# A hybrid encoder layer: the second sequence is scaled on ScalarE and transposed by channel tile, key rows are rotated after the fetch, weight splits are joined, and the output's products stand in another order

## The chip, the cores and the metric

The kernel runs on one core of a Trainium2 chip. The metric is the device time of one execution, in microseconds (us). TensorE is called PE, VectorE DVE, ScalarE ACT, GpSimd POOL and SyncE SP; SP issues nearly all DMAs, in order.

## The reference: what is computed

One encoder layer, for two independent sequences (a prompt and a sample) of 512 tokens and 1024 channels, all in float32.

```python
h = rms_norm(x, pre_g)
z = h @ w_in                                   # 6,560 columns, split into the parts below
(u_pool, c_q, kv_a, u_conv, u_four, g_pool, g_attn, g_conv, g_four, z_merge) = split(z)
y_pool = pool_mixer(u_pool, pool_w, pool_scale) * silu(g_pool)
y_attn = mla(c_q, kv_a, q_norm_g, w_uq, kv_norm_g, w_ukv) * silu(g_attn)   # 8 heads, rope on 32 key channels
y_conv = conv_module(u_conv, ...) * silu(g_conv)                          # 31 taps, layer norm, product
y_four = fourier_mixer(u_four, fourier_w) * silu(g_four)
gates = sigmoid((z_merge + gate_b).reshape(B, S, 4, D))
m = sum(gates[:, :, i] * (y_i @ w_up_i) for the four branches)
return x + rms_norm(m @ w_out, post_g)
```

## The kernel before

**Products.** Every product is made in three passes over numbers split in a high and a low half (`split`: ACT writes the high half, rounded to fp32r, then DVE or POOL subtracts it from the source and writes the low one); `mm3` issues the three passes, so that 8 channel tiles are 24 matmul instructions. Matmuls are up to 512 columns wide.

**Two sequences in one product.** Sequence 0 (F in the code) and sequence 1 (G) are taken together: the input projection has 50 channel tiles of 128, taken as 25 `PAIRS`, and each pair makes its 2 x 2 blocks (two channel tiles, two sequences) with seven products instead of eight. `group_units` names them `m1` to `m7`. Their right factors are the halves (channels 0 to 511, and 512 to 1023) of the hidden rows, transposed: B11 and B21 of sequence 0, B12 and B22 of sequence 1, and the sums T1 = B12 - B11, T2 = B22 - T1, T3 = B22 - B12, T4 = B21 - T2. `m1` and `m2` need sequence 0 alone, `m6` needs T2, and `m5`, `m7`, `m4`, `m3` need T1, T3, T4 and B22. Each left factor is a weight tile or a sum of weight tiles, split in the same way (`into`). The output product with `w_out` has seven products as well (`out_product(1)` to `(7)`, with left factors by `LEFT`, and `out_sums` for the sums of the merged rows).

**The front.** For each token tile of 128, `a_units` loads the rows, squares them (`stat`), scales them by the norm and the gain (`norm`), and transposes eight channel tiles on PE (`turn`). `b_units` is the projection on the query and key latents (416 columns wide, four tiles for each sequence); its evacuation norms them, rotates the 32 key channels (rope), and spills 480 columns to DRAM (`st`). The group stream follows, and beside it run the taps of the convolution: 120 DVE instructions on PSUM. Then come the attention, whose rows are fetched from DRAM by `c_units`, the merges (`merges(n)` for four branches), and the output, ended for each token tile by `half_out`, `residual` and `final`.

**The order.** A recorder keeps every instruction with what it reads and writes. `schedule` lists the bulk of PE's work in program order and gives the rest ("sides") start and end times from the table `PLAN`, relative to marks in the bulk. A planner then orders all instructions of each engine by these due times, an estimate of their durations, and the buffers that are free. `either` leaves it to the planner whether DVE or POOL takes an operation, `copied` whether ACT or DVE does. All DMAs stand in SP's order. Because the recorder issues every instruction at one place, all have line L182 in the profile, and groups are told apart by their tiles (`b` and `g` are SBUF buffers, `ps` PSUM, `s` small columns, `st` spilled rows, `in_wt` the projection's weights, `in_wv` the value weights).

The bulk around the output before the change:

```python
bulk.extend(out_product(1) + [out_gains()] + out_product(2))
merges(3, 1)
bulk.extend(out_sums(k) for k in range(4))
for n in (6, 7, 5):
    bulk.extend(out_product(n))
```

## Time and profile before

| what | value |
| --- | --- |
| median of 3 runs | 953.57 us |
| all runs | 953.54, 953.57, 1499.98 us |
| the profiled execution | 957.25 us |
| its span | 955.4 us |
| PE busy | 905.9 us (95%), 4,128 instructions |
| DVE, ACT, POOL busy | 724.1, 484.3 and 363.3 us |
| DMA | 130.90 MB in 55,842 packets |
| PE idle | 49.5 us |

The profile covers one execution; its span is from the first instruction to the last, and the execution's own time has 1.85 us around it. Times in rows are microseconds from the span's start. A row of the timeline has the start, the length, the engine, the line, the operation, the tiles written and read, and the number of instructions that were taken together; in brackets, how long the engine had been idle and what ended that.

### The profile page before, as it was taken

What the parts mean: (1) busy time and instruction counts of PE and PEld (TensorE: products, weight loads), DVE (VectorE), ACT (ScalarE), POOL (GpSimd) and SP (SyncE); (2) the same over time, 40 slices, a digit from 0 to 9 for tenths busy, and PEclk for the clock granted to TensorE, in tenths of its full rate; (3) what the DMA queues carried; (4) which work ended last, traced back from release to release, by engine and by line L of the source; (5) the groups of instructions that cost most, each with busy time, mean ns of one, the idle gap of its engine ahead of it and who ended that gap; (6) DMA issues with size and microseconds to landing.
All of it is one profiled execution on the core that took longest, in us unless ns stands there. A gap on an engine that the chain in (4) does not pass through costs nothing. (4 is left out here: it accounts for less than half of the span.)

```text
span 955.4 us, 12309 instructions
## 1 busy us (share of the span) xinstructions
PE 905.9 (95%) x4128; PEld 731.4 (77%) x4128; DVE 724.1 (76%) x1129; ACT 484.3 (51%) x907; POOL 363.3 (38%) x332
## 2 busy tenths in 40 slices
PE   5969999999999999999999998999999899999895
PEld 5967877877788887878888886878778677777684
DVE  5997999989655446477444375688989888888997
ACT  6734333334544544344444364665657787763343
POOL 4998433524212013142011021332533153359974
PEclk9998999999999999999999999899999999999898
DMA  7204024222343226335334234857842762640134
GB/s 276 99 32 153 14 99 142 90 109 99 133 155 121 78 69 212 122 111 187 105 138 137 94 117 118 278 187 244 285 151 67 224 238 80 220 143 22 43 113 176
DMA packets 55842, 130.90 MB, mean 137 GB/s; under 512 B 6882, under 2 KB 10211, under 8 KB 55267
## 3 DMA queue, kind: packets, MB, share of 16 engines
q1 hardware_dynamic: 55778, 130.13, 40.8%
q8 instruction: 32, 0.52, 0.2%
q14 instruction: 32, 0.25, 0.1%
HBM read 89.34 MB, written 37.62 MB: 133 GB/s over the span
## 5 line engine op out<-in xcount | busy, mean ns | idle before, releaser
L182 PE MATMUL ps<-b,b 128*128 128x512 f32 (+4 forms) x3476 | 824.7, 394 | 24.3 <-ACT b L182 10.2
L182 PEld LDWEIGHTS ps<-b,b 128*128 128x128 f32 (+2 forms) x3476 | 641.3, 189 | 175.4 <-ACT b L182 11.1
L182 DVE TENSOR_TENSOR b<-b,b 128x512 fp32r<-128x512 f32 (+4 forms) x187 | 169.0, 921 | 64.2 <-ACT b L182 60.4
L182 ACT ACTIVATE b<-b 128x512 fp32r<-128x512 f32 (+5 forms) x230 | 150.6, 673 | 125.4 <-PE ps L182 84.2
L182 POOL TENSOR_TENSOR b<-b,b 128x512 fp32r<-128x512 f32 (+3 forms) x82 | 123.3, 1515 | 166.0 <-ACT b L182 107.9
L182 ACT ACTIVATE g<-ps 128x512 f32<-128x512 f32 (+5 forms) x116 | 63.4, 549 | 132.8 <-PE ps L182 115.9
L182 DVE TENSOR_TENSOR g<-ps,g 128x512 f32<-128x512 f32 (+3 forms) x101 | 66.2, 658 | 74.8 <-ACT g L182 40.2
L182 DVE TENSOR_TENSOR b<-ps,b 128x512 fp32r<-128x512 f32 (+2 forms) x126 | 83.9, 682 | 9.4 <-ACT b L182 8.0
L182 ACT ACTIVATE b<-g 128x512 fp32r<-128x512 f32 x101 | 62.0, 628 | 49.4 <-DVE g L182 21.6
L182 DVE SCALAR_TENSOR_TENSOR ps<-b,half,ps 128x512 f32<-128x512 f32 x116 | 84.5, 750 | 1.6
L182 ACT ACTIVATE b<-ps 128x512 fp32r<-128x512 f32 (+2 forms) x117 | 67.8, 592 | 18.0 <-PE ps L182 15.9
L182 POOL TENSOR_TENSOR b<-g,b 128x512 fp32r<-128x512 f32 x37 | 52.0, 1411 | 53.2 <-ACT b L182 37.2
L182 POOL TENSOR_TENSOR b<-b,g 128x512 f32<-128x512 f32 x30 | 42.4, 1416 | 61.2 <-DVE g L182 47.4
L182 DVE TENSOR_TENSOR b<-g,b 128x512 fp32r<-128x512 f32 x64 | 51.3, 810 | 16.4 <-ACT b L182 16.0
L182 ACT ACTIVATE g<-g,half 128x512 f32<-128x512 f32 x48 | 34.8, 725 | 42.7 <-DVE g L182 42.6
L182 ACT ACTIVATE g<-ps,s 128x512 f32<-128x512 f32 x64 | 43.8, 685 | 24.7 <-DVE s L182 17.4
L182 POOL TENSOR_TENSOR b<-b 128x512 f32<-128x512 f32 (+2 forms) x25 | 33.0, 1320 | 39.4 <-DVE g L182 16.6
L182 PE MATMUL ps<-ident,g 128*128 128x128 f32 x280 | 43.0, 275 | 3.5 <-DVE b L182 2.2
L182 DVE TENSOR_REDUCE s<-ps 128x1 f32<-128x512 f32 x64 | 43.5, 682 | 2.5 <-PE ps L182 2.2
L182 DVE TENSOR_TENSOR b<-b 128x512 f32<-128x512 f32 (+4 forms) x50 | 38.6, 774 | 7.9 <-DMA b<-st 2.4
L182 PEld LDWEIGHTS ps<-ident,g 128*128 128x128 f32 x280 | 34.2, 141 | 13.6 <-issue 2.7
L182 POOL TENSOR_TENSOR g<-b,b 128x512 f32<-128x512 f32 x16 | 22.9, 1436 | 51.9 <-DMA b<-in_wt 21.3
(72 smaller groups left out, 567.4 us busy)
## 6 DMA issues: line engine op xcount, KB each, us to landing
st<-g SPq DMA_DIRECT2D x104, 256.0 KB, 2.1
b<-in_wt SPq DMA_DIRECT2D x50, 512.0 KB, 4.2
g<-st SPq DMA_DIRECT2D x100, 256.0 KB, 3.6
b<-in_x SPq DMA_DIRECT2D x15, 512.0 KB, 4.3
b<-in_wup SPq DMA_DIRECT2D x14, 512.0 KB, 5.8
b<-st SPq DMA_DIRECT2D x4, 1024.0 KB, 7.2
b<-in_wo SPq DMA_DIRECT2D x8, 512.0 KB, 4.5
out_y<-b SPq DMA_DIRECT2D x16, 256.0 KB, 2.0
```

The source lines that it names most:

```text
L182: getattr(engines[atom.eng], method)(*[real(x) for x in args], **{k: real(x) for k, x in kw.items()})
```

## The change

The change touches several parts, and all numbers of `PLAN` but a few are new.

1. *Sequence 1's rows.* `norm` scales them in place on ACT by the row's factor alone, without the gain. The new `turn1(k)` transposes the four token tiles of one channel tile into one PSUM bank, and its evacuation (`scaled_`, on ACT or DVE) multiplies by that channel's gain, which is a column of the new tile `gains`; T1 and T3 are made from 512 contiguous columns, and `sums(k)` makes T2 and T4 by channel tile too. `gains` is loaded by a DMA with channels on partitions.
2. *Powers.* The add ahead of a power moves from POOL to DVE, and the two powers of a latent tile are joined to one of two columns; the mean's factor goes into the Square's scale.
3. *Key rows* are spilled unrotated, 416 columns wide; `cn()` in `c_units` rotates all four token tiles at once after the fetch.
4. *Weights.* The two tiles of a pair are loaded into one buffer with their halves side by side, and split 1024 columns at a time (`ga`, `gb`, `gc`) and once 512 (`gd`).
5. *Group stream.* The first pair's `m1` and `m2` are put ahead of sequence 1's latent projection explicitly (`gl=1`).
6. *Output.* Product 7 comes first, on `s3`, made by `out_s3` as the last branch is merged; its four steps alternate with the sums; then come 6, which adds to two sums, 5, 4, 3.
7. *The end.* For sequence 0's last two token tiles, one DVE instruction replaces an ACT scale and an addition.

The diff's core:

```diff
+    def scaled_(out, x, c):
+        rec.choice(act=("activation", (out, x, AF.Copy), dict(scale=c)),
+                   dve=("tensor_scalar", (out, x, c, None), dict(op0=ALU.mult)))
...
-    def rsqrt_(out, ss, inv_n, eps):
+    def rsqrt_(out, ss, eps):
         n = ss.shape[-1]
         t = s_(n)
-        pool.tensor_scalar(t, ss, inv_n, eps, op0=ALU.mult, op1=ALU.add)
+        dve.tensor_scalar(t, ss, eps, None, op0=ALU.add)
         pool.tensor_tensor(out, t, mhalf[:, :n], op=ALU.pow)
...
+        def turn1(k):
+            def fn():
+                h, kk = divmod(k, 4)
+                name, sum_ = ("B12", "T1") if h == 0 else ("B22", "T3")
...
+                for tt in range(4):
+                    pe.transpose(pt[:, tt * P:(tt + 1) * P], st["x", tt][:, k * P:(k + 1) * P], ident)
+                scaled_(b, pt, gains[:, k:k + 1])
+                split(*row_of(name, kk), b)
+                if h == 0:
+                    hi, lo = row_of("B11", kk)
+                    either(t, hi.bitcast(F32), lo.bitcast(F32), ALU.add)
+                    either(t, b, t, ALU.subtract)
+                    st["b", kk] = b, t
+                else:
+                    either(t, b, st["b", kk][0], ALU.subtract)
+                    st["b", kk] = b, st["b", kk][1]
+                split(*row_of(sum_, kk), t)
+            return Unit(fn, 0.43)
...
             def norm():
+                if s:
+                    act.activation(st["x", tt], st["x", tt], AF.Copy, scale=st["rs", tt])
+                    return
...
-                dve.tensor_tensor(cn[:, 384:416], p[:, 384:416], kcs[:, tt, 0, :], op=ALU.mult)
...
-                dve.tensor_copy(cn[:, 432:448], cn[:, 384:400])
-            return [part(j) for j in range(4)] + [Unit(lambda: spill((s, "cn", tt), st.pop(("cn", tt))[:, :480]))]
+                copied(cn[:, 384:416], p[:, 384:416])
+                scaled_(cn[:, :256], p[:, :256], rs[:, 0:1])
+                scaled_(cn[:, 256:384], p[:, 256:384], rs[:, 1:2])
+            return [part(j) for j in range(4)] + [Unit(lambda: spill((s, "cn", tt), st.pop(("cn", tt))[:, :416]))]
...
             def cn():
...
+                k, u = t[:, :, 384:416], t[:, :, 448:480]
+                either(u[:, :, :16], t[:, :, 400:416], kcs[:, :, 1, :16], ALU.mult)
+                either(u[:, :, 16:], t[:, :, 384:400], kcs[:, :, 1, 16:], ALU.mult)
+                either(k, k, kcs[:, :, 0, :], ALU.mult)
+                either(k, k, u, ALU.add)
+                copied(t[:, :, 416:432], t[:, :, 400:416])
+                copied(t[:, :, 432:448], t[:, :, 384:400])
...
-        return (prod("ga0", "B11", "x", True, copy("m1")), prod("ga1", "B21", "y", True, total("m1", 0, i)),
-                prod("gb0", "T2", "x", False, copy("u2")), prod("gc0", "T1", "z", True, lambda p: None),
...
+        return (prod("ga", 0, "B11", "x", True, copy("m1")), prod("ga", 512, "B21", "y", True, total("m1", 0, i)),
+                prod("gb", 0, "T2", "x", False, copy("u2")), prod("gb", 512, "T1", "z", True, lambda p: None),
...
-    LEFT = {1: ("m", 0, 0), 2: ("m", 0, 1), 3: ("m", 0, 1), 4: ("m", 1, 1), 5: "s1", 6: ("m", 0, 0), 7: ("m", 1, 0)}
+    LEFT = {1: ("m", 0, 0), 2: ("m", 0, 1), 3: ("m", 0, 1), 4: ("m", 1, 1), 5: "s1", 6: ("m", 0, 0), 7: "s3"}
...
+                R["s1"] = R["m", 1, 0]
             a11, a12, a21, a22 = [R["m", s, i][:, k, :] for s in range(2) for i in range(2)]
-            s1 = R["s1"][:, k, :]
-            either(s1, a21, a22, ALU.add)
-            either(a21, a11, a21, ALU.subtract)
-            either(a11, s1, a11, ALU.subtract)
+            either(a21, a21, a22, ALU.add)
+            either(a11, a21, a11, ALU.subtract)
             either(a12, a12, a11, ALU.subtract)
...
-        elif n == 6:
-            dve.tensor_tensor(U[1][:, tt, :], p, U[1][:, tt, :], op=ALU.add)
...
+        elif n == 6:
+            for u in (U[7], U[1]):
+                dve.tensor_tensor(u[:, tt, :], p, u[:, tt, :], op=ALU.add)
...
         merges(3, 1)
-        bulk.extend(out_sums(k) for k in range(4))
-        for n in (6, 7, 5):
+        for k in range(4):
+            bulk.insert(marks_c[k] + k, out_s3(k))
+        us = out_product(7)
+        for k in range(4):
+            bulk.extend([out_sums(k), us[k]])
+        for n in (6, 5):
             bulk.extend(out_product(n))
...
+        side("tr1", "start", [G["turn1"](k + h) for k in range(4) for h in (0, 4)])
...
+        sync.dma_start(gains, a["pre"].rearrange("(k p) -> p k", p=P))
```

The instruction order of three places, before and after. PE, behind the latent projections of both sequences, with `ps_247_832` the second product of pair 0 (`m2`), and `b_244_820` and `b_249_852` the halves of T2; before:

```order
L182 MATMUL ps_247_832<-b_132_237,b_196_508 128x512
L182 MATMUL ps_247_832<-b_128_229,b_196_508 128x512 x2
L182 MATMUL ps_247_832<-b_132_237,b_196_508 128x512
L182 MATMUL ps_247_832<-b_128_229,b_196_508 128x512
L182 MATMUL ps_233_761<-b_244_820,b_260_897 128x512
L182 MATMUL ps_233_761<-b_249_852,b_260_897 128x512
L182 MATMUL ps_233_761<-b_244_820,b_260_897 128x512 x2
```

After, the last latent projection is `ps_242_772`; what follows are T1's product of pair 0 and the two first products of pair 1, whose left factor is `b_243_779`:

```order
L182 MATMUL ps_242_772<-b_138_265,b_207_565 128x416
L182 MATMUL ps_251_822<-b_211_581,b_185_481 128x512
L182 MATMUL ps_251_822<-b_216_606,b_185_481 128x512
L182 MATMUL ps_251_822<-b_211_581,b_185_481 128x512 x2
L182 MATMUL ps_251_822<-b_216_606,b_185_481 128x512
L182 MATMUL ps_251_822<-b_211_581,b_185_481 128x512 x2
```

Of the products that follow, these are the last rows of pair 1, and then the first of T2's product (`ps_205_556`, with T2 in `b_260_867` and `b_262_874`):

```order
L182 MATMUL ps_263_876<-b_132_238,b_243_779 128x512
L182 MATMUL ps_263_876<-b_128_230,b_243_779 128x512 x2
L182 MATMUL ps_263_876<-b_132_238,b_243_779 128x512
L182 MATMUL ps_263_876<-b_128_230,b_243_779 128x512
L182 MATMUL ps_205_556<-b_260_867,b_185_481 128x512
L182 MATMUL ps_205_556<-b_262_874,b_185_481 128x512
```

Before, T2's product stood right behind these; now 36 instructions stand between.

SP's queue around the value weights `in_wv`; before, where `b_611` and `b_624` are the query rows:

```order
L182 DMA st_176<-g_597_4462 128x512
L182 DMA b_611_4544<-b_608_4516 32x1024 x2
L182 DMA b_611_4544<-b_611_4544 64x1024
L182 DMA st_177<-g_609_4527 128x512
L182 DMA st_178<-g_614_4580 128x512
L182 DMA b_611_4544<-b_608_4516 32x1024 x2
L182 DMA b_624_4628<-b_608_4516 32x1024 x2
L182 DMA b_624_4628<-b_624_4628 64x1024
L182 DMA b_624_4628<-b_608_4516 32x1024 x2
L182 DMA b_642_4700<-in_wv 128x256
L182 DMA b_527_3742<-in_dft 128x516
```

After:

```order
L182 DMA b_671_4326<-in_wh 128x768
L182 DMA g_672_4335<-st_149 128x512
L182 DMA st_175<-g_663_4283 128x512
L182 DMA b_678_4371<-in_wh 128x768
L182 DMA st_176<-g_676_4360 128x512
L182 DMA b_678_4371<-in_wv 128x256
L182 DMA st_177<-g_679_4374 128x512
L182 DMA b_687_4421<-b_682_4388 32x1024 x2
L182 DMA b_687_4421<-b_687_4421 64x1024
L182 DMA st_178<-g_688_4427 128x512
L182 DMA b_687_4421<-b_682_4388 32x1024 x2
```

The value weights stood behind seven copies of query rows (`b<-b`); now they stand ahead of these.

DVE's last rows, for the last token tiles of sequence 0, with `g_1271_7203` and `g_1363_7136` the output's gain; before:

```order
L182 TENSOR_TENSOR b_1331_7434<-b_1331_7434,g_1271_7203 128x512
L182 TENSOR_TENSOR b_1331_7434<-ps_1430_8048,b_1331_7434 128x512
L182 SCALAR_TENSOR_TENSOR b_1331_7434<-b_1331_7434,s_1461_8319,b_1337_7465 128x512
L182 TENSOR_TENSOR b_1391_7697<-b_1391_7697,b_1337_7465 128x512
L182 TENSOR_TENSOR b_1331_7434<-b_1331_7434,g_1271_7203 128x512
L182 SCALAR_TENSOR_TENSOR b_1331_7434<-b_1331_7434,s_1463_8331,b_1296_7291 128x512
L182 TENSOR_TENSOR b_1391_7697<-b_1391_7697,b_1296_7291 128x512
```

After:

```order
L182 TENSOR_SCALAR s_1536_8205<-s_1480_7629 128x1
L182 TENSOR_TENSOR b_1404_7308<-b_1404_7308,g_1363_7136 128x512
L182 TENSOR_TENSOR b_1404_7308<-ps_1506_7912,b_1404_7308 128x512
L182 SCALAR_TENSOR_TENSOR b_1471_7590<-b_1471_7590,s_1537_8209,b_1413_7346 128x512
L182 SCALAR_TENSOR_TENSOR b_1404_7308<-b_1404_7308,s_1537_8209,b_1413_7346 128x512
L182 TENSOR_SCALAR s_1538_8216<-s_1481_7634 128x1
L182 TENSOR_TENSOR b_1404_7308<-b_1404_7308,g_1363_7136 128x512
L182 SCALAR_TENSOR_TENSOR b_1471_7590<-b_1471_7590,s_1539_8220,b_1410_7330 128x512
L182 SCALAR_TENSOR_TENSOR b_1404_7308<-b_1404_7308,s_1539_8220,b_1410_7330 128x512
```

The last tile's addition with the residual (`TENSOR_TENSOR`, the last row before) became a `SCALAR_TENSOR_TENSOR` that scales as well, and the power's add (`TENSOR_SCALAR s`) now stands on DVE.

More of the change, by code (lines that the diff above doesn't have):

```diff
@@ L532, in trunk_kernel @@
     cols, mhalf = cols[:, :107], cols[:, 107:]
-    half = const((P, 107), F32, "half")
+    gains = const((P, KD), F32, "gains")
     kcs = const((P, 4, 2, 32), F32, "kcs")
@@ L547, in trunk_kernel @@
         srcs["q", j] = (a["wq"][j], 832)
-    for i in range(50):
-        srcs["z", i] = (a["wt"][i], 1024)
     for i in range(10):
@@ L640, in fn, with row_of, sums @@
+        def row_of(name, k):
+            return [x[:, k, :] for x in R[name]]
+        def sums(k):
+            def fn():
+                if k == 0:
                     R["T2"], R["T4"] = [[b_([4, S], F32R), b_([4, S], F32R)] for _ in range(2)]
-                (t2, t1), t4 = st["b", tt], whole("B21", tt)
+                (t2, t1), t4 = st["b", k], g_()
+                hi, lo = row_of("B21", k)
+                either(t4, hi.bitcast(F32), lo.bitcast(F32), ALU.add)
                 either(t2, t2, t1, ALU.subtract)
-                split(*part_of("T2", tt), t2)
+                split(*row_of("T2", k), t2)
@@ L673, in fn @@
                 def fn():
-                    name = "B22" if k0 else "B12"
-                    if tt == 0 and s:
-                        R[name], R["T3" if k0 else "T1"] = [[b_([4, S], F32R), b_([4, S], F32R)] for _ in range(2)]
-                        if k0:
-                            st["hh"], st["hl"] = zip(R["B12"], R["B22"])
-                    elif tt == 0 and k0 == 0:
+                    if tt == 0 and k0 == 0:
                         hidden()
@@ L955, in fn @@
                 t = g_() if t is None else t
-                act.activation(t, p, AF.Tanh, scale=0.5, bias=half[:, GB + b * 8 + c:GB + b * 8 + c + 1])
+                act.activation(t, p, AF.Tanh, scale=0.5, bias=cols[:, GB + b * 8 + c:GB + b * 8 + c + 1])
                 spill((s, "g", b, c), t, act)
@@ L986, in fn @@
                     for j in js:
-                        w = half[:, CWT + c * 31 + j:CWT + c * 31 + j + 1]
+                        w = cols[:, CWT + c * 31 + j:CWT + c * 31 + j + 1]
                         if j == 0:
@@ L1039, in fn @@
                     t, y = g_(), g_()
-                    lg, lb = half[:, LG + c:LG + c + 1], half[:, LB + c:LB + c + 1]
+                    lg, lb = cols[:, LG + c:LG + c + 1], cols[:, LB + c:LB + c + 1]
                     act.activation(t, pt, AF.Tanh, scale=lg, bias=lb)
@@ L1258, in fn @@
                 v, w = st["half", 1 - q, tt], st["half", q, tt]
-                act.activation(v, v, AF.Copy, scale=r)
-                either(v, v, st["xr", tt][1 - q], ALU.add)
+                if s == 0 and tt > 1:
+                    dve.scalar_tensor_tensor(v, v, r, st["xr", tt][1 - q], op0=ALU.mult, op1=ALU.add)
+                else:
+                    act.activation(v, v, AF.Copy, scale=r)
+                    either(v, v, st["xr", tt][1 - q], ALU.add)
                 dve.scalar_tensor_tensor(w, w, r, st["xr", tt][q], op0=ALU.mult, op1=ALU.add)
@@ L1368, in whole, with prod @@
             evac(0, i2)(p)
-        def prod(key, r, bank, first, then):
+        def prod(key, o, r, bank, first, then):
             def part(j):
@@ L1519, in side @@
             sides.append((marks[mark] + t, marks[mark] + t + n, us))
-        def direct(s, n):
-            for i in PAIRS[n]:
-                bulk.extend(Fs[s]["z"](i, Fs[s]["tile"](i)))
         def merges(n, *ss):
@@ L1542, in schedule @@
         at("groups")
-        ln = [f["ln"]() for f in Fs]
-        late = [u for n in range(nd, len(PAIRS)) for i in PAIRS[n] for u in Fs[1]["z"](i, Fs[1]["tile"](i))]
-        bulk.extend(group_stream(range(nd), lambda n: [u for i in range(2) if n == q["pw%d" % i] for u in ln[i][1]], late))
+        bulk.extend(rest)
         at("tail")
@@ L1560, in schedule @@
         side("a1", "start", stagger(au1))
-        side("sums", "start", [G["sums"](tt) for tt in range(4)])
+        side("tr1", "start", [G["turn1"](k + h) for k in range(4) for h in (0, 4)])
+        side("sums", "start", [G["sums"](k) for k in range(4)])
         for s, F in enumerate(Fs):
@@ L1599, in const_unit @@
     def const_unit():
-        dve.tensor_scalar(half, cols, 0.5, None, op0=ALU.mult)
+        for c in (cols[:, GB:QG], cols[:, LG:PB], cols[:, CWT:]):
+            dve.tensor_scalar(c, c, 0.5, None, op0=ALU.mult)
+        sync.dma_start(gains, a["pre"].rearrange("(k p) -> p k", p=P))
     def got(j):
```

176 lines of the change are left out of this document (73 added, 103 removed).

## The prediction

> **What bounds the kernel now.** I read the page's busy times first, then the idle stretches of PE, the waits behind each, and the windows around them. (x: instructions; the bracket: idle time before the first, and what ended it. A window's row: from:to, length, busy time of PE, PEld, DVE, ACT and POOL, PE's granted clock, DMA share, GB/s.)
>
> ```profile
> PE 905.9 (95%) x4128; PEld 731.4 (77%) x4128; DVE 724.1 (76%) x1129; ACT 484.3 (51%) x907; POOL 363.3 (38%) x332
> 120.00:160.00 40.00, 39.03 (x168) 31.16 (x167) 39.56 (x63) 13.35 (x23) 13.03 (x11) 1.00 0.32 111
> ...
> 371.38 50.41 PE L182 MATMUL ps<-b,b 128*128 128x512 f32 x216 [0.48 <-ACT g L182]
> ```
>
> PE is the bound: 905.9 of 955.4 us. In the taps' window its granted clock is 1.00; it is lower in the gaps below. The undisturbed run of 216 products in 50.41 us gives the pitch of a 512-wide product, 0.233 us, and no step of the change touches it: before and after have 4,128 PE instructions. So the change can gain only in the 49.5 us in which PE is idle and in the stretches in which its granted clock is under full, and it can lose wherever another engine becomes late. Three gaps and the two ends hold most of that.
>
> The largest gap is at 64 us:
>
> ```profile
> 20.73 4.79 PE L182 MATMUL ps<-b,b 128*128 128x416 f32 x24
> ...
> 44.42 19.70 PE L182 MATMUL ps<-b,b 128*128 128x416 f32 x96
> 71.99 1.22 PE L182 MATMUL ps<-b,b 128*128 128x512 f32 x2 [7.88 <-ACT b L182]
> 74.63 25.63 PE L182 MATMUL ps<-b,b 128*128 128x512 f32 x98 [1.42 <-DVE b L182]
> 20.00:40.00 20.00, 19.17 (x116) 18.38 (x117) 19.53 (x38) 15.50 (x38) 18.24 (x22) 1.00 0.38 133
> 40.00:60.00 20.00, 20.00 (x111) 19.43 (x110) 20.00 (x47) 9.01 (x29) 18.72 (x19) 1.00 0.16 53
> ...
> 64.00:82.00 18.00, 8.71 (x23) 6.32 (x23) 15.64 (x25) 5.78 (x11) 16.34 (x17) 0.62 0.32 99
> ```
>
> PE ends the projections of both sequences and the first two products of pair 0 at 64.12 us, waits 7.88 us for the high half of T2 (ACT writes it) and 1.42 us for the low half, and then runs slow. In 64 to 82 it issues 23 products, 5.4 us at the pitch, in 8.71 busy us, at a mean granted clock of 0.62. Lost: 18 − 5.4 = 12.6 us, 9.3 of it idle and 3.3 by the clock. Behind the wait stand the two engines that make T1 to T4: from 20 to 60 us DVE is busy 39.53 of 40 us and POOL 36.96, while ACT is busy 24.51.
>
> The second gap is at 590 us:
>
> ```profile
> 574.47 11.73 SPq L182 DMA_DIRECT2D b<-b  x7
> 586.30 1.98 SPq L182 DMA_DIRECT2D b<-in_wv  x1
> 590.16 0.42 ACT L182 ACTIVATE g<-b 128x256 fp32r<-128x256 f32 x1 [6.23 <-DMA b<-in_wv]
> 591.81 0.96 PE L182 MATMUL ps<-b,b 128*128 128x512 f32 x3 [1.98 <-ACT g L182]
> 594.74 1.66 PE L182 MATMUL ps<-b,b 128*128 128x258 f32 x6 [1.96 <-ACT g L182]
> 588.00:604.00 16.00, 12.06 (x48) 9.81 (x46) 9.96 (x17) 9.06 (x19) 3.33 (x3) 0.68 0.66 176
> ```
>
> SP issues in order. Seven copies of query rows hold it for 11.73 us, and only then goes `in_wv`, the value weights. ACT waits 6.23 us for them, and PE stands for 1.98 and 1.96 us. With the clock at 0.68 over 588 to 604, PE has 12.06 us busy at a reduced rate: idle 3.94 us, and about 4 us more by the clock.
>
> The third is at 885 us, where output product 6 waits for its left factor, built from the merged sums by `out_sums`, then split:
>
> ```profile
> 885.52 0.73 PE L182 MATMUL ps<-b,b 128*128 128x512 f32 x2 [2.33 <-ACT b L182]
> 888.21 35.41 PE L182 MATMUL ps<-b,b 128*128 128x512 f32 x142 [1.95 <-DVE b L182]
> 884.00:897.00 13.00, 9.53 (x30) 7.32 (x31) 12.20 (x9) 3.15 (x5) 12.84 (x9) 0.74 0.01 2
> 850.00:900.00 50.00, 44.32 (x184) 34.23 (x183) 46.18 (x44) 18.35 (x36) 47.42 (x31) 0.93 0.11 39
> ```
>
> There are 30 products in 13 us, 7.0 us of work: 6 us lost, 4.3 idle, while DVE and POOL are busy 46.18 and 47.42 of 50 us.
>
> The end is a serial chain of one token tile:
>
> ```profile
> 944.13 1.52 PE L182 MATMUL ps<-b 128*128 128x512 f32 x6
> 947.17 0.68 DVE L182 TENSOR_TENSOR b<-ps,b 128x512 f32<-128x512 f32 x1
> 948.09 0.72 ACT L182 ACTIVATE b<-b,s 128x512 f32<-128x512 f32 x1 [1.55 <-POOL s L182]
> 948.71 0.58 ACT L182 ACTIVATE ps<-b 128x512 f32<-128x512 f32 x1
> 949.52 0.79 POOL L182 TENSOR_SCALAR s<-s 128x1 f32<-128x1 f32 x1 [1.47 <-ACT ps L182]
> 950.39 0.56 POOL L182 TENSOR_TENSOR s<-s,cols 128x1 f32<-128x1 f32 x1
> 950.98 0.75 DVE L182 SCALAR_TENSOR_TENSOR b<-b,s,b 128x512 f32<-128x512 f32 x1 [0.83 <-POOL s L182]
> 951.73 0.69 DVE L182 TENSOR_TENSOR b<-b,b 128x512 f32<-128x512 f32 x1
> ```
>
> **The change, part by part.** Sums are made against the profiled execution, 957.25 us (span 955.4 us and 1.85 around it); it stands 3.68 us above the median 953.57. I take the difference over to the median.
>
> *Front.* For sequence 1, the norm with its gain (DVE) becomes a scale on ACT, and the four token tiles of one channel tile are transposed into one bank, so that T1 to T4 are made by channel tile. The powers' adds move from POOL to DVE. DVE and POOL lose work here, and ACT, with 40 − 24.51 = 15.5 us free, gets it.
>
> ```profile
> L182 ACT ACTIVATE b<-g 128x512 fp32r<-128x512 f32 x101 | 62.0, 628 | 49.4 <-DVE g L182 21.6 <-PE ps L182 17.9 <-POOL g L182 7.1
> L182 ACT ACTIVATE b<-ps 128x512 fp32r<-128x512 f32 x94 | 54.5, 592 | 14.7 <-PE ps L182 13.9 <-POOL g L182 0.2
> L182 ACT ACTIVATE g<-ps,s 128x512 f32<-128x512 f32 x64 | 43.8, 685 | 24.7 <-DVE s L182 17.4 <-DVE g L182 2.3 <-issue 2.2
> L182 ACT ACTIVATE b<-b 128x1024 fp32r<-128x1024 f32 x14 | 14.6, 1050 | 1.5 <-PE ps L182 1.4
> L182 ACT ACTIVATE b<-b 128x1024 f32<-128x1024 f32 x7 | 7.4, 1058 | 2.6 <-DMA b<-in_x 1.9 <-DVE b L182 0.3 <-POOL s L182 0.2
> ```
>
> ACT's new work, from the first transposed block of sequence 0 (18.72 us in the profile) to the last high half of sequence 1's rows: 6 splits from PSUM at 0.59, 4 squares over 1024 with their accumulator at 1.25, 4 row scales at 1.06 (from the `128x1024` square), 2 wide weight halves at 1.05, 6 evacuations scaled by channel at 0.685, 11 splits at 0.628, 3.1 us of small squares and 1.3 us of small scales: 30.3 us, to 49 us if ACT never waits. That is the bound from below.
>
> PE, from 20.73 us, has 72 projections of sequence 0 (0.2 each, from 4.79 us for 24), ten blocks of four transposes (some 3.6 us), 24 products of pair 0 (5.6) and, as an estimate, two stalls of 0.9 us before sequence 1's projections: 46 us. ACT is then 3 us from its end, and the first projections read the early channel tiles, so I take no wait. 96 projections at 0.2 end at 66.5 us, 2.4 later than the profile's 64.12. Now 36 products that need no T2 (T1's of pair 0, two of pair 1) follow: 8.4 us, until 74.9 us. T2 was ready at 72 to 74 us with POOL and DVE full; with their load lightened I take 71. So PE goes on: by 82 us it has done (82 − 66.5)/0.233 = 66 products instead of 23. **−43×0.233 = −10.0 us**, bounds −12.6 (nothing lost) and +15 (rival 1).
>
> *Gains.* The scale by channel needs the gain with channels on partitions: 1,024 separate elements, queued behind the weights of pair 0. The nearest row is the small `corr`:
>
> ```profile
> corr<-in_corr SPq DMA_DIRECT2D x1, 16.0 KB, 1.8
> ```
>
> 128 rows in 1.8 us; eight times as many descriptors one after the other give 14.4 us, side by side 1.8. The weights ahead of it:
>
> ```profile
> 28.82 1.29 POOL L182 TENSOR_TENSOR g<-b 128x512 f32<-128x512 f32 x1 [0.43 <-DMA b<-in_wt]
> ```
>
> They are there at 28.8 us, so the gain comes at 31 to 43 us; the first scaled evacuation, behind some 64 projections (12.8 us from 20.73) and the first transposes, is near 37 us. I take 0, near the lower end; upper end +6, worked out as a rival. [...]
>
> *Value weights.* In SP's row `in_wv` now stands before the query copies, behind a load of `in_wh` and two spills. The 6.23 us wait falls away and with it up to 8 us. Behind it the query copies land no later, since they waited for their own data; but the attention before them is also moved by the retuned due times. **−6 us**, bounds −8 and 0.
>
> *Key rows.* Eight small DVE instructions per token tile become six operations per sequence over `128x4x16` and `128x4x32`, behind the fetch, and what waits there is the key product, queued behind them on PE. No row has such a shape; the nearest are `128x512` operations, DVE 0.86 and POOL 1.47 us, as upper ends, and nothing as the lower: six give 0 to 9 us of latency a sequence, and rows are fetched some 10 us ahead. I take 0, upper end +2.
>
> *Output.* Product 7 comes first, on a left factor (`s3`) that is made while the last branch is merged; one of the four sums goes, and each remaining sum stands directly ahead of a part of product 7.
>
> ```profile
> L182 DVE TENSOR_TENSOR b<-b,b 128x512 f32<-128x512 f32 x33 | 33.5, 1021 | 1.7 <-POOL b L182 1.0 <-ACT b L182 0.3
> L182 POOL TENSOR_TENSOR b<-b,b 128x512 f32<-128x512 f32 x15 | 22.1, 1479 | 10.0 <-DVE b L182 8.6 <-ACT b L182 0.8
> ```
>
> Twelve operations behind the merge become eight beside 48 products (11.2 us); at 1.02 on DVE and 1.48 on POOL the two need about 8 × 1.25/2 = 5 us, and PE has work for 11.2. Product 6 now adds twice on DVE: 4 × 0.68 us more, while DVE has about 4 us free of the 50; that is why I don't take all. **−5 us**, bounds −6 and +2.
>
> *End.* Of the last chain, ACT's square no longer stands behind the scale (0.72); the add moves from POOL to DVE (0.79 and its way to the pow, about 0.7 less); the addition before it is about 0.8 earlier: **−2.2 us**, bounds −3 and 0. What is late next is the DVE's own pair of operations (0.75 and 0.69), now two STT, and the DMA out.
>
> *Wide splits and weights.* Four splits per pair take the place of seven.
>
> ```profile
> L182 DVE TENSOR_TENSOR b<-b,b 128x512 fp32r<-128x512 f32 x134 | 113.7, 862 | 55.2 <-ACT b L182 53.0 <-PE ps L182 2.1
> L182 DVE TENSOR_TENSOR b<-b,b 128x1024 fp32r<-128x1024 f32 x10 | 13.3, 1342 | 3.9 <-ACT b L182 3.8
> ```
>
> 1.342 for 1024 columns against 2 × 0.862: DVE saves some 0.38 us for each, and ACT 2×0.628 − 1.05 = 0.2. PE covers this, so it is worth 0 at 100% PE; but from 100 to 200 us the taps keep DVE busy (39.56 of 40 us in the window above), and fewer POOL choices put weights on DVE. Its work by pair is, counted from the order, 19.7 to 24.9 us in the tap stage against 19.6 on PE. I take **0**, bounds −2.4 (PE's gaps in that stage) and +5.
>
> Sum: −10 − 6 − 5 − 2.2 = **−23.2**, so 957.25 − 23.2 = 934.05 profiled and 953.57 − 23.2 = **930.4**.
>
> **Rivals.** (1) *Slower:* ACT becomes the front's bound. In 20 to 60 us it did only 61% of what it could, since it waited for DVE and PE; with the same share, 30.3/0.61 = 49.7 us put its end at 68 instead of 49. PE would stand from 46 to 68, and pay 4 us by the clock: projections end at 91.6 instead of 66.5, +25.1 on the forecast, **955.5**. It loses against before when ACT ends after about 65 us. For it: the chain PE, ACT, DVE of every channel tile is serial, and each transpose needs all four token tiles. Against: ACT's waits in 20 to 40 us are short (15.50 of 20 busy). 0.06.
> (2) *A smaller hole:* ACT ends at 55; PE waits 8 us with seq. 1's projections, 4 more by the clock; the front's gain goes: 953.57 − 13.2 = **940.4**. 0.13.
> (3) *Late gains:* 43 us for 37; 6 us idle and 4 of clock: **940.4**, too. 0.05.
> (4) *No gain in the tap or output stage:* DVE lags there: +5 by the wide splits, the output's −5 kept half, and half of the value weights' −6: **941**. 0.07.
> (5) *All stalls go*, the small ones too:
>
> ```profile
> 750.00:800.00 50.00, 46.96 (x230) 35.88 (x229) 41.25 (x73) 38.21 (x75) 21.18 (x16) 1.00 0.63 209
> ```
>
> PE is idle 3.0 us of 50 here, and the bounds of front, wv and output give 2.6 + 2 + 1 more: 930.4 − 8.6 = **921.8**. 0.10.
>
> (6) *The clock does not come back with the gaps*: what the slow stretches lose beside their idle time (3.3, about 4 and 1.7 us) stays, as another cause would leave it. The sum becomes −6.7 − 2 − 3.3 − 2.2 = −14.2: **939.4**. Against it: the clock falls in these three places, and each has a gap just ahead. 0.04. [...]
> (7) *The change does only what its words say of ACT, and the retuned order brings the old gaps elsewhere:* DVE and POOL are as late for T2, the output's sums are late by the merge. Only the end's 2.2 and 4 of `in_wv` remain: **947**. 0.05.
>
> **How the numbers follow.** The forecast itself, 925 to 938, has 0.50, the rivals 0.50 as given. About 2% is what a measurement of this kernel tells from no change: below 934.5 is faster. Of the forecast's 0.50 I put 0.45 there, and with the 0.10 of (5) this makes 0.55; slower by over 2% (above 972.6) would take (1) with more still: 0.02; within 2% 0.43. The range goes from 921, just under (5), to 947, (7); outside are (1) and the edges of the bounds.
>
> **What would show it.** Front: PE's chain of sequence 1's projections without a gap over 1 us and a clock near 1 between 60 and 82 us; T2's wait gone or below 1 us. ACT's projection part: its last scaled evacuation by 50 us; over 55 is (2), a wait on `in_pre` is (3). Value weights: `in_wv` lands before ACT is free. Output: no PE idle over 1 us between the last merge and product 6. End: under 7.7 us between PE's last product and the end of the span. Tap stage: PE idle in 100 to 200 us not above 2.4 us. The prediction is wrong if one of the moved due times opens a gap of several microseconds that before does not have, at the attention stage (550 to 850 us) above all, of which I worked out only the value weights.

## The result and the profile after

The changed kernel takes **930.61 us** (median of 4 runs, 927.70 to 931.72) against 956.45 us before: a ratio of 0.9735, with a 95% interval from 0.9683 to 0.9787. The 956.45 is the median of four executions of which one, at 1499.98 us, was slow and is left out of the ratio; the others took 953.54, 953.57 and 959.33 us, and the series of 7 to 31 executions that were measured beside the experiments have medians from 955.93 to 957.22. The forecast was 930.4, with 921 to 947 as its range. The profiled execution took 927.70 us, with a span of 925.9.

The page after, its busy times first, then PE's granted clock by fortieths of the span:

```profile
PE 895.3 (97%) x4128; PEld 723.8 (78%) x4128; DVE 708.9 (77%) x1036; ACT 488.8 (53%) x863; POOL 327.6 (35%) x279
...
PEclk9999999999999999999999999999999999999998
```

PE has the same 4,128 instructions, in 895.3 busy us instead of 905.9. Its granted clock is 1.00 until 921.2 us, in the last fortieth and behind the last product. Of the 10.6 us, 10.2 are what the slow clock had cost before and 0.4 are less work; and PE's idle time went from 49.5 to 30.6 us. The clock's record begins only at 15.9 us before and 16.6 us after. The first 24 projections, at 11 to 19 us, took 7.06 and 6.72 us, and 24 later ones, at 20.73 us in the kernel before, took 4.79; if the clock was slow there too, that stands in the work of both.

PE's timeline at the front:

```profile
44.25 6.45 PE L182 MATMUL ps<-b,b 128*128 128x512 f32 x30
51.30 26.10 PE L182 MATMUL ps<-b,b 128*128 128x416 f32 x126 [0.60 <-DVE g L182]
78.77 31.45 PE L182 MATMUL ps<-b,b 128*128 128x512 f32 x134 [1.37 <-ACT g L182]
```

The window that stands against 8.71 busy us (x23) at a clock of 0.62 before:

```profile
64.00:82.00 18.00, 16.63 (x75) 13.63 (x74) 15.19 (x14) 9.09 (x20) 16.95 (x11) 1.00 0.27 83
```

The last 78 of sequence 1's 96 projections, the 36 products and the 12 of T2's product run as one row of 126 until 77.40 us. No wait for T2 is left. What is left is a wait of 1.37 us for ACT, which copies T2's product out of PSUM:

```profile
76.65 1.06 ACT L182 ACTIVATE b<-b 128x1024 fp32r<-128x1024 f32 x1 [4.11 <-POOL b L182]
77.61 0.61 ACT L182 ACTIVATE b<-g 128x512 fp32r<-128x512 f32 x1
78.14 0.58 ACT L182 ACTIVATE g<-ps 128x512 f32<-128x512 f32 x1
```

PE ended T2's product at 77.40. The copy (78.14) stands in ACT's queue behind a wide weight half, which had waited 4.11 us for POOL, and one more split.

SP's queue around the value weights, which now go at 554 us, ahead of the copies:

```profile
554.08 2.00 SPq L182 DMA_DIRECT2D b<-in_wv  x1
...
559.05 2.11 SPq L182 DMA_DIRECT2D b<-b  x3
```

The output, where the two waits and the slow clock were, in PE's timeline and then in the window:

```profile
849.61 37.61 PE L182 MATMUL ps<-b,b 128*128 128x512 f32 x159
```

```profile
850.00:900.00 50.00, 49.97 (x216) 39.80 (x215) 47.84 (x56) 21.85 (x43) 40.41 (x26) 1.00 0.26 85
```

The first row starts where its window was cut; from there PE runs 159 products in 37.61 us without a wait, out of the last merge and on through product 7, while DVE is busy 47.84 of 50 us.

The end, in rows picked from the engines' timeline:

```profile
917.00 0.86 PE L182 MATMUL ps<-b,b 128*128 128x512 f32 x3
917.90 0.69 DVE L182 TENSOR_TENSOR b<-ps,b 128x512 f32<-128x512 f32 x1
918.62 0.60 ACT L182 ACTIVATE ps<-b 128x512 f32<-128x512 f32 x1 [1.81 <-DVE b L182]
919.83 0.21 DVE L182 TENSOR_SCALAR s<-s 128x1 f32<-128x1 f32 x1
920.12 0.92 POOL L182 TENSOR_TENSOR s<-s,cols 128x1 f32<-128x1 f32 x1 [1.91 <-DVE s L182]
921.07 1.41 DVE L182 SCALAR_TENSOR_TENSOR b<-b,s,b 128x512 f32<-128x512 f32 x2 [0.44 <-POOL s L182]
```

For the comparison I take PE's **lost time**: its idle time, plus its busy time multiplied by one minus the granted clock, instruction by instruction. What is left of the span is the work, 895.7 us before and 895.3 after, so places can be set side by side by how much work precedes them. All these sums are taken from the instructions of the two profiled executions.

| place | before: idle + clock | after | difference | forecast |
| --- | --- | --- | --- | --- |
| start, the first 22 us | 10.0 + 0 | 11.1 + 0 | +1.1 | 0 |
| front, T2 | 9.4 + 3.6 | 1.4 + 0 | -11.6 | -10 |
| value weights | 3.9 + 4.1 | 1.5 + 0 | -6.5 | -6 |
| output, behind the last merge | 5.4 + 2.4 | 0 + 0 | -7.8 | -5 |
| end, behind the last product | 9.8 | 8.1 | -1.7 | -2.2 |
| all others | 11.1 | 8.5 | -2.6 | 0 |
| sum | 59.7 | 30.6 | -29.1 | -23.2 |

With the 0.4 us less of work this is, to 0.1 us, the difference of the two profiled executions, 957.25 and 927.70. Of the two, the first was 0.8 us above its kernel's median as measured later (956.45), the second 2.9 below; the medians are 25.8 apart.

### The profile page after: what moved, and what is told of

Its sections match the earlier page's. It is cut to its first block, busy times and chain, and to the rows that moved or that the text cites. A ratio compares the mean times of both kernels' runs of the same rounds, so it can differ in the third digit from the quotient of the medians.

```text
span 925.9 us, 12037 instructions
## 1 busy us (share of the span) xinstructions
PE 895.3 (97%) x4128; PEld 723.8 (78%) x4128; DVE 708.9 (77%) x1036; ACT 488.8 (53%) x863; POOL 327.6 (35%) x279
## 4 chain that ended last, share of the span: by engine, by line
PE 62%; DVE 3%; ACT 2%; DMA 2%; issue 1%; POOL 1%; SPq 0%; POOLq 0%; DVEq 0%; ACTq 0%
PE ps L182 62%; DVE b L182 2%; ACT b L182 1%; DVE g L182 1%; ACT g L182 1%; DMA b<-in_wup 1%; DMA g<-in_wo 1%; DMA st<-g 0%; POOL b L182 0%; DMA g<-st 0%; SPq L182 0%; DVE s L182 0%; POOLq L1800 0%; POOL s L182 0%; DVEq L1800 0%
## 5 line engine op out<-in xcount | busy, mean ns | idle before, releaser
L182 PEld LDWEIGHTS ps<-b,b 128*128 128x128 f32 (+1 forms) x3464 | 632.5, 187 | 155.9 <-DVE b L182 9.1
L182 ACT ACTIVATE b<-b 128x1024 fp32r<-128x1024 f32 (+7 forms) x159 | 139.2, 891 | 130.5 <-PE ps L182 47.3
L182 DVE TENSOR_TENSOR b<-b,b 128x1024 fp32r<-128x1024 f32 (+4 forms) x134 | 154.9, 1169 | 38.7 <-ACT b L182 38.4
L182 DVE TENSOR_TENSOR g<-ps,g 128x512 f32<-128x512 f32 (+4 forms) x101 | 66.3, 659 | 71.4 <-PE ps L182 38.7
L182 ACT ACTIVATE g<-ps 128x512 f32<-128x512 f32 (+6 forms) x111 | 59.4, 538 | 98.3 <-PE ps L182 85.8
L182 DVE TENSOR_TENSOR b<-ps,b 128x512 fp32r<-128x512 f32 (+2 forms) x130 | 86.6, 683 | 12.4 <-ACT b L182 11.6
L182 POOL TENSOR_TENSOR b<-b 128x512 f32<-128x512 f32 (+4 forms) x40 | 55.6, 1390 | 100.2 <-DVE b L182 38.3
L182 DVE SCALAR_TENSOR_TENSOR ps<-b,cols,ps 128x512 f32<-128x512 f32 x116 | 84.7, 752 | 1.6
L182 POOL TENSOR_TENSOR b<-b,b 128x512 fp32r<-128x512 f32 (+4 forms) x34 | 56.0, 1670 | 22.9 <-ACT b L182 13.2
L182 ACT ACTIVATE g<-ps,s 128x512 f32<-128x512 f32 (+2 forms) x76 | 48.5, 644 | 19.6 <-DVE s L182 12.1
L182 DVE TENSOR_TENSOR b<-b 128x512 f32<-128x512 f32 (+5 forms) x61 | 51.5, 845 | 7.3 <-PE ps L182 3.1
```

What stands on the lines that cost most here:

```text
L182: getattr(engines[atom.eng], method)(*[real(x) for x in args], **{k: real(x) for k, x in kw.items()})
```

## The experiments

Each kernel was measured beside the kernel before on the same chip; the ratio to it is given with its interval. The changed kernel's 930.61 us are from a series of their own, so a difference to it is one between two series. "Lost" is as above, and is read from one profiled execution of each kernel.

**1. The order at the front alone.** Before, with `sums=(33, 8)` replaced by `sums=(35, 8)`.

> The kernel before with one number of PLAN changed: the sums T2 and T4 are due at 35 us instead of 33. The planner then puts 36 products that need no T2 (T1's product of pair 0 and two of pair 1) ahead of T2's product, as in the changed kernel; the operations of sequence 1's rows stay as before. Theory A (order): the front gap went because PE had 36 other products to do while T2 was made. Then the PE time lost between 64 and 82 us falls from 13.0 us (9.4 idle, 3.6 by the clock) to under 5, and the whole to about 944 to 948. Theory B (load): it went because ACT took the scaling and DVE and POOL had less to do. Then T2 only comes later here, 9 us or more stay lost, and the time is unchanged.

Measured: 953.36 us, ratio 0.9959 (0.9939 to 0.998). The front loses 10.5 us (7.1 idle, 3.4 by the clock) instead of 13.0.

```profile
74.07 0.72 PE L182 MATMUL ps<-b,b 128*128 128x512 f32 x2 [1.78 <-ACT b L182]
77.10 6.92 PE L182 MATMUL ps<-b,b 128*128 128x512 f32 x22 [2.30 <-POOL b L182]
84.71 3.06 PE L182 MATMUL ps<-b,b 128*128 128x512 f32 x12 [0.69 <-ACT g L182]
89.77 20.61 PE L182 MATMUL ps<-b,b 128*128 128x512 f32 x81 [2.00 <-DVE g L182]
```

Neither theory holds by itself. The 36 products are ahead, but T2's halves now come at 74.07 and 77.10 us, and behind them two evacuations are late as well (0.69 and 2.00).

**2. The value weights alone.** Before, with `v0=(-4.84, 5.23)` replaced by `v0=(-8, 5.23)`.

> The kernel before with one number of PLAN changed: the value units of sequence 0 are due 3 us earlier (v0 -8 instead of -4.84), which puts the load of the value weights ahead of the query copies in SP's queue. If the late load alone made the gap at 590 us, the 8.0 us lost there (3.9 idle, 4.1 by the clock) fall to under 2 and the time to about 946. Rival: the query copies or another operand are just as late; then 4 us or more stay lost and the time is above 950.

Measured: 954.67 us, ratio 0.9975 (0.9945 to 1.0005). The place loses 1.8 us instead of 8.0, as expected, and the slow clock is gone there; the time shows 1.6 of the 6.2 us. The profiled execution lost 1.7 us to the slow clock at a later wait that cost the kernel before none, and 1.6 more at the start; and behind the place stand waits of 1.34 us at 624 us and 1.43 us at 857 us, where before has 0.44 and 0.31. The mechanism is shown by the place; its effect on the time alone is not.

**3. The output's order alone.**

The core of the edit:

```diff
-        bulk.extend(out_sums(k) for k in range(4))
-        for n in (6, 7, 5):
+        for k in range(4):
+            bulk.insert(marks_c[k] + k, out_s3(k))
+        us = out_product(7)
+        for k in range(4):
+            bulk.extend([out_sums(k), us[k]])
+        for n in (6, 5):
```

> The kernel before with the output's part of the change alone: product 7 first on s3, then 6, 5, 4, 3, and sums in place. My own step, -5: DVE and POOL stay full, so a rest of 2 us of the 7.8 lost at 885 us stays. Theory: the sums then stand beside product 7 and nothing is left, -7.8, about 946. Rival: the wait moves into product 7 itself, since s3 and the split stand on the same two engines; then 4 us or more are lost at that place and the time is 950 or more.

Measured: 956.76 us, ratio 1.0027 (0.9995 to 1.0059). Nothing is lost ahead of product 7, but 4.2 us idle and 3.4 by the clock behind it:

```profile
897.93 7.45 PE L182 MATMUL ps<-b,b 128*128 128x512 f32 x24 [2.46 <-DVE b L182]
906.16 0.73 PE L182 MATMUL ps<-b 128*128 128x512 f32 x2 [0.78 <-ACT b L182]
907.90 3.98 PE L182 MATMUL ps<-b 128*128 128x512 f32 x10 [1.01 <-DVE b L182]
```

The rival has the size right, 7.6 us against 7.8, but the wait is not in product 7: it moved to the product behind. This execution took 962.69 us, 5.9 more than the median, and its end behind the last product lost 12.7 us where before lost 9.8; so the place shows the wait that moved, and the time alone shows that nothing was won.

**4. The clock.** Before, with 34 products that nobody reads ahead of T2's. `at` is the last PE instruction ahead of T2's product, `bank` a free PSUM bank, and `NFILL` is 34; the search for the two is not shown.

```diff
             rec.emit(rec.atoms[n], engines, tile_of)
+            if p == at:
+                _, (_, lh, rh), _ = rec.atoms[n].calls[-1]
+                for _ in range(NFILL):
+                    nc.tensor.matmul(tile_of_bank(bank), lh.real(tile_of), rh.real(tile_of), start=True, stop=True)
```

> The kernel before with 34 extra products of 512 columns, whose result nobody reads, put on PE right ahead of T2's product, where PE is idle for 7.9 us; nothing else in the order moves. Theory C (the clock falls because PE is idle): the 34 take 7.9 us in the gap, the clock stays at 1.00 over 64 to 82 us, and the 3.6 us that the slow clock cost are gone: the time falls by about 3.5. Rival D (something else lowers the clock there): it is at 0.5 all the same, the 34 products then take longer than the gap and the time rises by 3 us or more.

Measured: 954.68 us, ratio 0.9978 (0.9956 to 0.9999).

```profile
64.00:82.00 18.00, 15.58 (x67) 12.02 (x66) 16.56 (x30) 8.15 (x16) 15.73 (x19) 1.00 0.33 113
```

PE's waits for T2 in the same execution:

```profile
76.95 0.73 PE L183 MATMUL ps<-b,b 128*128 128x512 f32 x2 [1.76 <-ACT b L183]
78.34 12.50 PE L183 MATMUL ps<-b,b 128*128 128x512 f32 x53 [0.66 <-DVE b L183]
```

The clock stays at 1.00 where it was 0.62, at the same place and with the same instructions before and behind, although 2.42 us of waits remain. That PE's idle time of 9.3 us lowered the clock is shown for this gap. The total fell by 1.6 us rather than 3.5 (medians); this profiled execution lost 1.7 us to the slow clock at its start, where the kernel before lost none.

**5. The operations without the numbers.** The changed kernel with before's PLAN.

> The changed kernel with all its operations, but with the numbers of PLAN that the kernel before had (those that only the changed kernel has are kept). After the first four runs, each single move of before gained 3 us or less. Theory B2 (the operations): with lighter DVE and POOL the waits are short wherever the order puts them; the time stays under 938. Theory A2 (the numbers): without the new due times T2's product stands first again, and the query copies stand ahead of the value weights; the front and the 590 us gap lose 6 us or more each, and the time is 945 or more.

Measured: 959.07 us, ratio 1.0029 (1.0009 to 1.005). This kernel does not compute the layer: the second of its two outputs is off by a relative 0.048, and why is not known. So its time is that of this order of the work, and not of a kernel that could be used. As far as it goes, theory A2 holds: 14.1 us are lost at the front, 6.5 at the value weights, 6.9 at the output.

```profile
75.85 34.33 PE L182 MATMUL ps<-b,b 128*128 128x512 f32 x137 [11.71 <-ACT b L182]
```

**6. The scale on DVE.**

```diff
-                    act.activation(st["x", tt], st["x", tt], AF.Copy, scale=st["rs", tt])
+                    dve.tensor_scalar(st["x", tt], st["x", tt], st["rs", tt], None, op0=ALU.mult)
```

> The changed kernel with sequence 1's row scale on DVE (a tensor_scalar of 128x1024) instead of ACT; four such instructions, some 1.1 us each by the 0.56 us of the 512-wide one. If ACT's taking them over is what closed the front gap, DVE's 4.4 us more come back as a wait of 3 us or more for T1, T2 or sequence 1's rows, and with the slow clock about 5. If it was the order (36 products ahead of T2's) and the other operations, the front loses at most 1 us more, and the time stays within 2 us of the changed kernel's 930.6.

Measured: 931.13 us, ratio 0.9742 (0.9705 to 0.9779), 0.5 us from the changed kernel. The four scales took 0.75 to 1.07 us each on DVE, 3.3 in all instead of the 4.4 expected. In the profiled execution, the slowest of the four at 933.74 us, the front does lose more, 5.6 us against 1.4:

```profile
74.61 3.12 PE L182 MATMUL ps<-b,b 128*128 128x512 f32 x11 [1.98 <-DVE b L182]
79.61 30.55 PE L182 MATMUL ps<-b,b 128*128 128x512 f32 x124 [1.89 <-ACT g L182]
```

By the time ACT's taking over the scale is worth nothing that can be told; by the one trace it may be worth up to 4 us at its place. The two don't agree, and this stays open.

**7. Narrow splits.** The changed kernel with two splits of 512 columns for each of 1024.

> The changed kernel with its weights split 512 columns at a time (seven splits per pair, as before) instead of 1024. My step took 0 for the wide splits, with bounds -2.4 and +5. If that was right, the time stays within 2 us. If the wide splits matter, DVE has 0.38 us a split more, 1 us a pair and 25 us over the stream, which it does not have while the taps run: PE then waits 3 us or more between 80 and 260 us.

Measured: 930.97 us, ratio 0.974 (0.9709 to 0.9771). Over the taps (90 to 260 us of work) PE lost 3.4 us. That is over the 3 us of the second expectation, but the changed kernel loses 2.6 there itself: by the time the wide splits are worth nothing that can be told here, as the step said.

**8. The old output in the changed kernel.** Products 6, 7, 5 and the four sums as before.

> The changed kernel with the output's products and sums in the order of before (6, 7, 5, then 4 and 3). The reordering put into the kernel before only moved the wait from product 6 to the place behind product 7. If the output's order is needed all the same, the 5.4 us of idle time and 2 to 3 by the clock come back behind the last merge: about 938. Rival: the wait is gone by the other numbers of PLAN and by the lighter DVE; then the time stays within 2 us of 930.6.

Measured: 944.13 us, ratio 0.9883 (0.9849 to 0.9916). 14.4 us are lost (9.4 idle, 5.0 by the clock), more than the 7.8 of the kernel before:

```profile
865.46 0.73 PE L182 MATMUL ps<-b,b 128*128 128x512 f32 x2 [2.41 <-ACT b L182]
...
888.21 4.03 PE L182 MATMUL ps<-b,b 128*128 128x512 f32 x10 [4.55 <-DVE b L182]
```

The reordering that brought nothing in the kernel before is worth 13.5 us of time with the new numbers.

**9. T2's product first in the changed kernel.** `sums=(39.97, 3.84)` replaced by `sums=(33, 8)`.

> The changed kernel with one number put back: the sums T2 and T4 due at 33 us over 8 instead of 39.97 over 3.84, so that T2's product stands ahead of the 36 other products again. In the changed kernel T2 is complete at 75.5 us, hardly other than before (74.6). Theory A (order): the 36 products (8.4 us) were the cover; PE stands 6 us or more for T2, with some 2 to 4 us by the clock, and the time is about 940. Theory B (load): with T2's sums earlier in the order and DVE and POOL lighter, T2 is complete by 70 us, the front loses under 4 us, and the time is under 934.

Measured: 943.63 us, ratio 0.9868 (0.9838 to 0.9898). Theory A holds:

```profile
78.88 31.44 PE L182 MATMUL ps<-b,b 128*128 128x512 f32 x123 [12.68 <-ACT b L182]
```

T2 comes at 78.88 us though its sums stand earlier and DVE and POOL have less to do; PE stands 12.68 us, and 2.8 go to the clock. Before, with the same due times for the sums, T2 came at 71.99, and in experiment 5, with all of before's numbers, at 75.85: with the new operations T2 comes later, not earlier.

**10. The numbers of the tail.** Before's operations, the reordered output, the new numbers but for the front's.

> The kernel before with the output's reordering and with the changed kernel's numbers for the tail (attention, branches, output) and for the planner as a whole, but with the front's numbers and all other operations as before. If numbers and reordering together close the output's gap, with no help from the new operations, nothing is lost there (7.8 before, 14.4 in the changed kernel with the old output), the 590 us gap is under 2, the front still loses 13, and the time is about 942. If the new operations are needed, 5 us or more are lost behind the last merge, and the time is 948 or more.

Measured: 946.23 us, ratio 0.9895 (0.9866 to 0.9924), between the two expectations. At its places the first one holds: 1.1 us lost at the output, 1.6 at the value weights, 11.6 at the front. In this execution 3.1 us more were lost late in the taps, and its work was 2.7 us more, for which I have no cause.

```profile
72.19 1.22 PE L182 MATMUL ps<-b,b 128*128 128x512 f32 x2 [7.38 <-ACT b L182]
```

**11. The gain in one load.** The changed kernel loads sequence 0's gain row in two halves, which the list of the change does not name; here it is one load again.

```diff
-        for c in (slice(0, 512), slice(512, D)):
-            sync.dma_start(gb[:, c], a["pre"][c].partition_broadcast(P))
+        sync.dma_start(gb, a["pre"].partition_broadcast(P))
```

> The changed kernel with sequence 0's gain row loaded by one DMA, as before, instead of two halves; nothing else in the order moves. In the changed kernel the second half came late (a wait of 1.58 us) and the first projection began at 12.48 us instead of 11.12. If the halves cause this, the start loses 1.1 us less and the time is about 929.5; if it is the other loads of the start, nothing changes (within 0.3 us).

Measured: 929.90 us (927.39 to 931.84), ratio 0.9725 (0.97 to 0.975). PE's start, first in the changed kernel, then here:

```profile
9.71 1.12 PE L182 MATMUL ps<-ident,b 128*128 128x128 f32 x4 [1.22 <-DVE b L182]
12.48 6.72 PE L182 MATMUL ps<-b,b 128*128 128x416 f32 x24 [1.65 <-DVE b L182]
```

```profile
7.92 1.97 PE L182 MATMUL ps<-ident,b 128*128 128x128 f32 x8 [7.92 <-DVE b L182]
10.68 7.38 PE L182 MATMUL ps<-b,b 128*128 128x416 f32 x24 [0.80 <-DVE b L182]
```

The start loses 9.3 us instead of 11.1 in these two executions; the medians, 0.7 us apart with intervals that overlap, don't tell it from no change.

**12. Order alone.** Experiment 10 with `sums=(35, 8)`.

> All that order can do without the new operations: the kernel before with the output's reordering, the new numbers for the tail and the planner, and the sums due at 35 us, which puts 36 products ahead of T2's. The run with the tail's numbers stands at 946.2 with 11.6 us lost at the front. If the order closes the front too, 4 us or less are lost there and the time is 938 or less. If the front needs the changed kernel's other operations as well (channel tiles, the scale on ACT, adds on DVE, joined powers), 8 us or more stay lost, as when the sums' due time was changed alone (10.5), and the time is 942 or more.

Measured: 937.39 us, ratio 0.9801 (0.9768 to 0.9833). The time is that of the first expectation, the front's loss that of the second: 8.3 us, 6.6 of it idle.

```profile
71.78 0.71 PE L182 MATMUL ps<-b,b 128*128 128x512 f32 x2 [1.80 <-ACT b L182]
75.09 6.92 PE L182 MATMUL ps<-b,b 128*128 128x512 f32 x22 [2.60 <-POOL b L182]
82.69 3.07 PE L182 MATMUL ps<-b,b 128*128 128x512 f32 x12 [0.69 <-ACT g L182]
87.24 22.97 PE L182 MATMUL ps<-b,b 128*128 128x512 f32 x98 [1.47 <-DVE g L182]
```

So 18.7 of the 25.8 us between the medians come from numbers and the output's reordering, without the other new operations. The front loses 6.9 us more here than in the changed kernel (8.3 - 1.4), which is about the 6.8 us between the two medians; but that the front accounts for them is not shown, since the start loses 2.0 us less here, the output and the end lose 2.0 more, and the work is 2.4 us more. Nor is it shown that the new operations win the 6.9 us: of the front's numbers this kernel has only `sums` moved, and the new operations with the old front's numbers but for `sums`, or the other way round, were not tried.

## Why the prediction was right, and where its reasons were not

**The total.** Right, at 930.4 for 930.61, and the places of the terms were right. That it fits to 0.2 us is luck. The sum of -23.2 was 5.9 us too small against the two profiled executions and 2.6 too small against the two medians (25.8); the 953.57 that it was taken from was 2.9 below the median as measured later, and the two errors cancel.

**Front (-10, measured -11.6).** The timetable held: ACT's last high half of sequence 1's rows was done at 47.9 us (row 46.59; 49 forecast), and the projections began at 47.1 (46) and ended at 66.3 (66.5). That last fit is luck again: 96 projections at 0.2 from 46 give 65.2, and the 66.5 of the forecast does not follow from its own terms. The -10 was counted in products done by 82 us, and by that count it is -10.0: PE had done 58.2 us of work by then before, and 68.2 after. The table's -11.6 is the place at T2 alone; 1.6 us of it are lost again at the start and at small waits ahead of it. The window of 20 to 40 us, then ACT's timeline and DVE's:

```profile
20.00:40.00 20.00, 18.58 (x111) 17.24 (x109) 16.36 (x31) 19.37 (x41) 10.77 (x11) 1.00 0.44 151
```

```profile
35.73 0.69 ACT L182 ACTIVATE g<-ps,gains 128x512 f32<-128x512 f32 x1 [0.36 <-ACT b L182]
...
46.59 1.30 ACT L182 ACTIVATE b<-g 128x512 fp32r<-128x512 f32 x2
...
68.23 3.41 ACT L182 ACTIVATE b<-g 128x512 fp32r<-128x512 f32 x6
```

```profile
71.98 3.48 DVE L182 TENSOR_TENSOR b<-g,b 128x512 fp32r<-128x512 f32 x2
```

The step that failed is "with their load lightened I take 71" for T2. Its high halves end at 71.6 and its last low half on DVE at 75.5 us, hardly other than before (74.6). DVE and POOL did have less to do early (16.36 and 10.77 busy us of 20 to 40, from 19.53 and 18.24), but where T2 is made they are as busy as before. From 60 to 82 us, before and then after:

```profile
60.00:82.00 22.00, 12.62 (x39) 9.00 (x38) 18.38 (x32) 8.78 (x18) 20.10 (x23) 0.69 0.29 92
60.00:82.00 22.00, 20.63 (x96) 17.60 (x95) 19.19 (x19) 10.77 (x25) 20.95 (x13) 1.00 0.34 109
```

The chain also starts later: with channel tiles no channel tile can be transposed and scaled until all four token tiles are there, and ACT's first scaled evacuation is at 35.73. That this is what takes back the lighter load is argued, and no run tries it alone. T2 met its product because 36 products, 8.4 us, stood ahead of it; with T2 first it is a 12.68 us wait (experiment 9). The order alone (experiment 12) still waits 4.4 us for T2's two halves and 2.2 for the evacuations behind. There T2's low half is ready at 75.1 us, as early as here, but PE is at T2's product at 69.98, and here at 74.47: part of the cover is that PE comes later.

**Value weights (-6, measured -6.5).** Right, and for the reason given: experiment 2 takes away 6.2 us at this place with one number. ACT waited 11.2 us for the value weights before, and 0.2 in the changed kernel.

**Output (-5, measured -7.8, outside its bounds of -6 and +2).** Mis-sized, and the reason was half of it. Of the loss I had counted 6 us; by the trace it was 5.4 idle and 2.4 by the clock, since the wait of 1.09 us at 874 us belongs to it. The step "twelve operations become eight beside 48 products" would have given the gain to the kernel before as well, and there it gave none (experiment 3). It needs the new due times too (10 against 3, and 8 for the other side). Which of the numbers does it was not tried: planner's window, the final due time and the branches' due times changed together.

**End (-2.2, measured -1.7).** The addition came earlier by more than I took: it starts 0.04 us after PE's last product instead of 1.52. But the add on DVE won nothing: from the end of ACT's accumulator to the last DVE pair it is 1.73 us, and was 1.56. The add itself takes 0.21 us on DVE instead of 0.79 on POOL, but it starts 0.48 us behind the accumulator instead of 0.10, since DVE still works on the pair of the tile before, and the pow takes 0.92 instead of 0.56, for which I have no cause. From the last DVE instruction to the end of the span it is 3.43 us instead of 3.00. So the sign "under 7.7 us" between PE's last product and the end of the span did not come: it is 8.1.

**Costs taken as nothing.** Wide splits: right (experiment 7). Gains: the load landed 5.5 us after its issue at 23.28, inside the bounds of 1.8 and 14.4, and was there before the first evacuation at 35.73. Nothing in any run shows the 1,024 elements to have cost time. Key rows: no wait of PE above 1 us is left between 590 and 680 us. Tap stage: 0.9 us of PE's idle time in 100 to 200 us, under the 2.4 of the sign. Not in the sum at all was the start, +1.1 us, where the gain's second half came late; that this costs time is not shown (experiment 11). DVE's wait for it, and then SP's issue of `gains` with the time to its landing:

```profile
8.90 0.75 DVE L182 SCALAR_TENSOR_TENSOR b<-b,s 128x512 f32<-128x512 f32 x1 [1.58 <-DMA b<-in_pre]
```

```profile
23.28 0.60 SPq L182 DMA_DIRECT2D gains<-in_pre  x1
...
DMA to landing us min/median/max: 5.5/5.5/5.5
```

**Rivals.** (1), (2) and (3) did not come about, since ACT and the gains were in time; nor (4). Nor did (5): front and output came near its bounds or over them, but 30.6 us of idle time are left, 2.0 of them from 740 to 770 us, where it counted on the 3.0 of before to go. Against (6): none of the 10.2 us by the clock in the three gaps is left, and experiment 4 shows the idle time as the cause for one of them. (7) had it the wrong way round: the new due times are what closed the gaps, and the operations without them won nothing (experiment 5, with its second output off).

## What to carry to other kernels

When a planner sets the order, an operation's saving and its due time are one change: here the operations without the new numbers won nothing, numbers and the output's reordering without the other operations gave 937.39 us, both 930.61, and a reordering worth nothing in one setting was worth 13.5 us in the other. To account for such a change, set lost time against work done, place by place; it shows a wait that has moved where the time alone shows nothing. And a cover is counted in products that stand ahead of the late operand, not in how much lighter the engines are that make it.

## What the runs showed of the hardware

In the trace of the kernel before, the granted clock falls to 0.50 at each of the three gaps: for 13.65 us from 67.05, for 10.24 from 592.70 and for 6.83 from 886.25, which are 4, 3 and 2 times 3.41 us. The three gaps cost 10.2 us by the clock on top of 18.7 us idle.

How long PE waits does not by itself tell whether its clock falls. At 592.70 us it fell behind one gap of 1.98 us, 0.89 us of work later and ahead of the second gap of 1.96. In the same trace it stayed at 1.00 over four waits of 2.61 us in all between 761 and 766 us, and in experiment 4 over the waits of 1.76 and 0.66 us for T2. Why one wait is followed by a slow stretch and another is not, no run shows.
